# Banded attention inside an encoder layer: operands split once at projection, near maximum kept negated, far sums taken by a column of ones, far scores in alternating order

## The chip, the core and the metric

The kernel runs on one core of a Trainium2 chip. The core has five engines with instruction streams of their own: TensorE (PE; its weight loads are listed apart as PEld), VectorE (DVE), ScalarE (ACT), GpSimd (POOL) and SyncE (SP, which here only issues DMAs). Each engine takes its instructions in a fixed order. The order is made when the program is built: a scheduler takes the operations as the code emits them, with earlier ones preferred, and lays each on its engine where it expects the operands to be ready. Data lie in SBUF (128 partitions), in PSUM (where PE writes) and in DRAM.

The metric is the device time of one execution in microseconds. The kernel before takes 2369.29 us (median of three runs, 2369.18 to 2370.75).

## What is computed

The layer is a feed-forward block, a mixer and a second feed-forward block over 1024 tokens of width 1024. The mixer has eight attention heads of width 64 and an RWKV-7 group that shares the input projection. The attention is the part that the change touches:

```python
DILATED_PATTERNS = ((128, 1), (512, 4), (2048, 16))
...
    for window, dilation in DILATED_PATTERNS:
        o, l = _dilated_attention(q, k, v, window, dilation)   # o: softmax output, l: log of its denominator
...
    wts = jax.nn.softmax(jnp.stack(lses, axis=0), axis=0)
    o = jnp.sum(wts[..., None] * jnp.stack(outs, axis=0), axis=0)
    o = o * lax.rsqrt(jnp.mean(o * o, axis=-1, keepdims=True) + NORM_EPS)
```

In a pattern, query i sees the keys i + dilation*j with |j| up to window/(2*dilation). The mix of three softmaxes by their denominators equals one softmax over all keys of the three patterns, where a key that two patterns share counts twice.

## The kernel before

**Stages.** First feed-forward block; low-rank and value projections; projection and turning of queries and keys (`project_attention`); attention (`attention`); projection of the RWKV streams (`project_rwkv`); preparation and scan of the RWKV blocks; output projection; second feed-forward block. Attention and `project_rwkv` don't depend on each other, so the scheduler may lay the products of the second (tile `zr`, L510) between those of the first on PE. `project_rwkv` goes over eleven column blocks: the four key blocks, three of the four r blocks (the first was done in `project_attention`), and then, between preparations, the four value blocks. Each takes 48 products of 512 columns, 528 in all. Their weights come in pieces of 64 KB (`zraw`) on SP's queue.

**Two halves of a number.** A float32 operand is used as a high part (rounded to the fast format `F32R`) and a low part (the rest), made by a copy on ACT and a subtraction on DVE. The near scores are q times k from stacked halves: `sq` holds the high part of q in one half of the partitions and its low part in the other; `kh` holds the high part of k twice, `kl` its low part twice. One product of `sq` with `kh` and one with `kl` (L685, L686) then make the whole score. `stacked` (L654) builds the three for a head from the float32 q and k of its pair of heads, with three ACT copies (L660 to L662) and three DVE subtractions (L663 to L665) over 64 partitions by 1024.

**Turning (L472 to L489).** For each of eight token tiles of k and then of q: 24 products of 512 columns, a copy out of PSUM on ACT (L477), the rotation in three DVE operations (L480 to L482), four transposes on PE (L486), a DVE copy (L488) and a store to DRAM by POOL's queue (L489).

**Far keys (`far`, L619).** Dilation 16 splits tokens into 16 residues of 64. For each residue, PE multiplies 64 queries with 64 keys, read with a step of 16 elements (L626). The result of residue r goes to rows 0 to 63 of the PSUM tile for r below 8, and to rows 64 to 127 from 8 on. DVE takes the maximum and subtracts it, ACT takes the exponential, DVE sums (L632); PE transposes (L638); ACT copies; PE multiplies with the values (L644); output, maximum and sum go to DRAM as `n3` and come back by tokens as `far`.

**Near keys (`near`, L668).** Dilations 1 and 4 stay within 256 tokens. For each of eight query tiles, up to 640 keys: `scores` makes the products, and a DVE operation (L687) adds a table of logarithms of counts and takes the running maximum at once. DVE negates the maximum (L690), ACT takes exp(s - m) and sums (L691). `turn` transposes on PE (L700) and copies (L701, shared between ACT and DVE); `values` multiplies with the values (L707). The emission is staggered: scores of tile t, turn of t-1, values of t-2. At a head's end eleven small DVE and ACT operations (L720 to L730) merge the near and far softmax; a DVE product (L732) then empties the PSUM tile `po` that the next head's values need.

**Heads.** While head h runs, the code emits the three parts of `far(h + 1)` at tiles 1, 3 and 5, and `stack(h + 1)` at tile 4. Scores use two PSUM tiles (tag `s`, shared with the far work); `sq`, `kh` and `kl` have two buffers each, that is two heads.

Of the kernel before, what the change touches and what calls it, by code (L numbers as in the profile page):

```python
# [31 lines left out]
def _ap(src, off, pat):  # L32
    return bass.AP(tensor=src.tensor, offset=src.offset + off, ap=pat)
# [130 lines left out]
class _Kernel:  # L164
# [290 lines left out]
    def project_attention(self, p, psum, x, streams):  # L455
# [12 lines left out]
        for b in (1, 0):  # L468
            hl = self.columns(p, b * 512, 512, W[b], bufs=11)
            if b:  # L470
                self.load(rope.rearrange("p t a b c -> p t (a b c)"), self.io["k_rope"].rearrange("(t p) c -> p t c", p=128))
            for t in range(NT):  # L472
                ps = psum.tile([128, 512], F32, name="zq", tag="d", bufs=5)
                self.token_major(ps, x, t, hl)
                ts = slice(t * 128, t * 128 + 128)
                z = zz[t % 6]
                A.activation(z.rearrange("p a b c -> p (a b c)"), ps, AF.Copy, scale=HD ** -0.5 if b == 0 else 1.0)  # L477
                cs = rope[:, t]
                o, y = zo, zy
                V.tensor_tensor(o, z, cs[:, None, 0].to_broadcast([128, 8, 2, 32]), op=OP.mult)  # L480
# [138 lines left out]
    def far(self, psum, p, h, q, k, v3):  # L619
# [4 lines left out]
        ps = psum.tile([128, NT, 64], F32, name="s3", tag="s", bufs=2)  # L624
        for r in range(16):
            T.matmul(ps[row(r // 8), r % 8, :], q[hs, r::16], k[hs, r::16], start=True, stop=True)  # L626
        n3 = p.tile([128, NT, 66], F32, name="n3", tag="n3", bufs=1)
        s = p.tile([128, NT, 64], F32, name="sb3", tag="sb3", bufs=1)
        V.tensor_reduce(out=n3[:, :, 64], in_=ps, op=OP.max, axis=AX.X)
        V.tensor_tensor(s, ps, n3[:, :, 64:65].to_broadcast([128, NT, 64]), op=OP.subtract)  # L630
        A.activation(s, s, AF.Exp)
        V.tensor_reduce(out=n3[:, :, 65], in_=s, op=OP.add, axis=AX.X)  # L632
        yield
# [6 lines left out]
        yield  # L640
        po = [psum.tile([128, 4, 64], F32, name="po3" + tag, tag=tag, bufs=2) for tag in "st"]
        for r in range(16):
            c, g, j = r // 8, r % 8 // 2, r % 2
            T.matmul(po[j][row(c), g, :], e[row(j), g, row(c)], v3[row(j), c * 4 + g, hs], start=True, stop=True)  # L644
        for j in range(2):
            A.copy(n3[:, j::2, 0:64], po[j])
        for c in range(2):
# [5 lines left out]

    def stacked(self, p, h, q, k):  # L654

        V, A = self.nc.vector, self.nc.scalar
        hs, os = slice(h % 2 * 64, h % 2 * 64 + 64), slice(64 - h % 2 * 64, 128 - h % 2 * 64)
        sq, kh, kl = (p.tile([128, S], F32R, name=n, tag=n) for n in ("sq", "kh", "kl"))
        q, k = q[hs], k[hs]
# [3 lines left out]
        V.tensor_tensor(sq[os], q, sq[hs], op=OP.subtract)  # L663
        V.tensor_tensor(kl[hs], k, kh[hs], op=OP.subtract)
        V.tensor_tensor(kl[os], k, kh[hs], op=OP.subtract)  # L665
        return sq, kh, kl

    def near(self, psum, p, h, sq, kh, kl, v, far, between):  # L668

        nc, V, A, G, T = self.nc, self.nc.vector, self.nc.scalar, self.nc.gpsimd, self.nc.tensor  # L670
        hs = slice(h % 2 * 64, h % 2 * 64 + 64)
        m, nm, d, M, c12, c3 = (p.tile([128, NT], F32, name=n, tag=n) for n in ("m", "nm", "dn", "M", "c12", "c3"))
        po = psum.tile([128, NT, 64], F32, name="po", tag="o", bufs=1)
# [3 lines left out]
        def scores(t):  # L677
# [4 lines left out]
            for c in range(0, n, 512):  # L682
                e = min(n, c + 512)
                ps = psum.tile([128, 512], F32, name="s12", tag="s", bufs=2)
                T.matmul(ps[:, :e - c], sq[:, qs], kh[:, k0 * 128 + c:k0 * 128 + e], start=True, stop=False)  # L685
                T.matmul(ps[:, :e - c], sq[:, qs], kl[:, k0 * 128 + c:k0 * 128 + e], start=False, stop=True)  # L686
                V.tensor_tensor_reduce(out=s[:, c:e], in0=ps[:, :e - c], in1=bias[:, c:e], scale=1.0,  # L687
                                       scalar=m[:, t:t + 1] if c else -3e38, op0=OP.add, op1=OP.max,
                                       accum_out=m[:, t:t + 1])
            V.tensor_scalar(nm[:, t:t + 1], m[:, t:t + 1], -1.0, None, op0=OP.mult)  # L690
            A.activation(s[:, :n], s[:, :n], AF.Exp, bias=nm[:, t:t + 1], accum_out=d[:, t:t + 1])  # L691

# [25 lines left out]
        f = far  # L718
        fm, fd = f[:, :, 64], f[:, :, 65]
# [20 lines left out]
    def attention(self, psum, p):  # L740
        X, F, ST = {}, {}, {}

        def load(pr):
            v3 = p.tile([128, 8, 128], F32, name="v3", tag="v3", bufs=1)
            for j in range(2):
                self.load(v3[j * 64:j * 64 + 64],
                          _ap(self.v_att, j * 512 + pr * 128, [[16 * 512, 64], [2 * 512, 8], [1, 128]]))
            vn = p.tile([128, NT, 128], F32, name="vn", tag="vn")
# [12 lines left out]
        def stack(h):  # L761
            q, k, _, _ = X[h // 2]
            ST[h] = self.stacked(p, h, q, k)

# [334 lines left out]
    def constants(self):  # L1099
# [13 lines left out]
        self.ws_d = [self.dram(f"ws{j}", [4, NM, 128, 512]) for j in range(2)]  # L1113
        self.v_att, self.ya_d = self.dram("va", [S, 512]), self.dram("ya", [S, 512])
        self.n3_d = [self.dram(f"n3{j}", [S, 66]) for j in range(2)]
        self.lr_d = {nm: [self.dram(f"{nm}{d}", [4, 128, S]) for d in range(2)] for nm in "wa"}
# [319 lines left out]
```

## Time and profile before

| what | value |
|---|---|
| median of three runs | 2369.29 us |
| span of the profiled execution | 2367.7 us |
| mean granted clock of TensorE | 0.960 |
| products of the q and k projection | 801.5 to 902.9 us |
| first far scores | 918.4 us |
| first and last value product of the heads | 942.0 and 1163.5 us |
| products `zr` | 923.8 to 1261.0 us |
| first product of the RWKV preparation (L830) | 1208.2 us |

A row of a group gives the line in the code, the engine, the operation, the output and inputs by name, the shape, the count; then busy time in us and mean duration in ns; then the idle time of the engine before it and what ended that idle time. A row of the timeline begins with the start and the length in us. On PE a float32 product stands as two rows, so 16 far products are 32 rows; a run of rows is merged with its count.

### The profile page before, as it was taken

The page shows a single profiled execution, that of the slowest core. Times are in us where ns is not written, and L with a number is a line of the kernel's source. Part 1 is how long each engine was busy: PE and PEld are TensorE (multiplying, and loading weights), DVE is VectorE, ACT ScalarE, POOL GpSimd, SP SyncE. Part 2 cuts the span into 40 slices and gives each one's busy share as a digit, 9 for nine tenths or more (in the row PEclk, how much of TensorE's full clock was granted, in tenths as well). Part 3 has the DMA queues.
Part 4 walks back from the last instruction along what each step waited for, and adds up shares of the span by engine and source line. Part 5 has one row for each costly group of instructions (what it writes and reads, how often), then busy time and mean ns, then how long its engine had stood idle before and what let it go on. Part 6 is the DMA issues. An engine that isn't in the chain of part 4 may idle for free. (4 is left out here: it accounts for less than half of the span.)

```text
span 2367.7 us, 39507 instructions
## 1 busy us (share of the span) xinstructions
PE 2212.2 (93%) x14532; PEld 1784.9 (75%) x14532; DVE 1782.8 (75%) x2957; ACT 1034.4 (44%) x1958; POOL 608.7 (26%) x732
## 2 busy tenths in 40 slices
PE   6999999999999998999995889988799999999997
PEld 4788888878877676788774767765678888887886
DVE  8899999865676344667568767837889999987565
ACT  4322333354676413666545545445442333235453
POOL 6244443400000010111102242432334344441000
PEclk8999999999999998999996798989989999999999
DMA  5354445486652514322369676577534544447655
GB/s 156 107 174 151 170 146 170 167 266 193 220 185 98 193 42 134 91 81 71 94 161 223 165 183 176 151 208 256 178 95 168 174 167 154 169 153 265 195 188 181
DMA packets 359381, 386.04 MB, mean 163 GB/s; under 512 B 74258, under 2 KB 265618, under 8 KB 359188
## 3 DMA queue, kind: packets, MB, share of 16 engines
q1 hardware_dynamic: 308512, 276.43, 38.8%
q0 software_dynamic: 30320, 94.44, 11.3%
q10 hardware_dynamic: 20356, 12.66, 1.9%
q8 instruction: 114, 1.87, 0.3%
q14 instruction: 79, 0.65, 0.1%
HBM read 257.53 MB, written 125.89 MB: 162 GB/s over the span
## 5 line engine op out<-in xcount | busy, mean ns | idle before, releaser
L186 ACT ACTIVATE wh<-raw 128x512 fp32r<-128x512 f32 (+1 forms) x273 | 167.8, 626 | 264.1 <-DVE raw L62 95.0
L187 DVE TENSOR_TENSOR wl<-raw,wh 128x512 fp32r<-128x512 f32 (+1 forms) x273 | 277.6, 1020 | 3.1 <-ACT wh L186 2.0
L81 PE MATMUL gu<-xh,wh 128*128 128x512 f32 x704 | 277.9, 395 | 0.9 <-ACT xh L186 0.8
L81 PE MATMUL gu<-xl,wh 128*128 128x512 f32 x704 | 276.3, 393 | 0.0
L81 PE MATMUL gu<-xh,wl 128*128 128x512 f32 x704 | 276.2, 392 | 0.0
L415 PE MATMUL pd<-gl,gwh 128*128 128x512 f32 x616 | 240.4, 390 | 3.1 <-DVE gl L187 3.1
L415 PE MATMUL pd<-gh,gwh 128*128 128x512 f32 x616 | 239.6, 390 | 0.5 <-DVE row L86 0.5
L415 PE MATMUL pd<-gh,gwl 128*128 128x512 f32 x616 | 239.7, 389 | 0.0
L86 DVE TENSOR_TENSOR row<-gu,row 128x512 f32<-128x512 f32 x308 | 206.4, 682 | 23.2 <-PE gu L81 22.4
L187 DVE TENSOR_TENSOR gwl<-graw,gwh 128x512 fp32r<-128x512 f32 (+1 forms) x176 | 117.0, 667 | 129.7 <-ACT gwh L186 127.5
L116 POOL DMA_DIRECT2D d_hid<-row x154 | 84.7, 551 | 470.6 <-DVE row L114 444.2
L186 ACT ACTIVATE gwh<-graw 128x512 fp32r<-128x512 f32 (+1 forms) x176 | 101.4, 576 | 190.5 <-PE pd L415 162.2
L81 PEld LDWEIGHTS gu<-xh,wh 128*128 128x128 f32 x704 | 133.9, 190 | 29.5 <-ACT xh L186 2.0
L81 PEld LDWEIGHTS gu<-xl,wh 128*128 128x128 f32 x704 | 133.8, 190 | 27.9
L81 PEld LDWEIGHTS gu<-xh,wl 128*128 128x128 f32 x704 | 133.3, 189 | 27.5
L415 PEld LDWEIGHTS pd<-gl,gwh 128*128 128x128 f32 x616 | 115.6, 188 | 28.5 <-DVE gl L187 4.9
L415 PEld LDWEIGHTS pd<-gh,gwh 128*128 128x128 f32 x616 | 115.5, 188 | 25.6 <-DVE row L86 0.8
L415 PEld LDWEIGHTS pd<-gh,gwl 128*128 128x128 f32 x616 | 115.6, 188 | 23.8
L94 ACT ACTIVATE row<-row 128x512 f32<-128x512 f32 x44 | 27.9, 633 | 223.9 <-DVE row L86 216.4
L187 DVE TENSOR_TENSOR gl<-raw,gh 128x512 fp32r<-128x512 f32 x160 | 112.9, 717 | 15.7 <-ACT gh L186 15.4
L145 POOL TENSOR_TENSOR ws<-ws 128x512 f32<-128x512 f32 x88 | 114.4, 1300 | 1.2
L186 ACT ACTIVATE gh<-raw 128x512 fp32r<-128x512 f32 x160 | 98.0, 621 | 32.2 <-DMA raw<-in_ffn_w_down_dram 21.1
(356 smaller groups left out, 5353.4 us busy)
## 6 DMA issues: line engine op xcount, KB each, us to landing
d_hid<-row POOLq DMA_DIRECT2D x154, 256.0 KB, 2.5
graw<-d_hid SPq DMA_DIRECT2D x132, 256.0 KB, 3.0
raw<-in_ffn_w_gate_dram SPq DMA_DIRECT2D x88, 256.0 KB, 3.1
raw<-in_ffn_w_up_dram SPq DMA_DIRECT2D x88, 256.0 KB, 3.3
ws<-in_ffn_w_down_dram SPq DMA_DIRECT2D x88, 256.0 KB, 4.5
d_ws<-ws POOLq DMA_DIRECT2D x88, 256.0 KB, 2.3
raw<-d_ws SPq DMA_DIRECT2D x88, 256.0 KB, 2.7
raw<-in_ffn_w_down_dram SPq DMA_DIRECT2D x66, 256.0 KB, 3.3
```

The lines of the kernel that those rows point to most:

```text
L81: self.K.nc.tensor.matmul(ps, a[:, k, :], b[:, k, :], start=(k == 0 and i == 0), stop=(k == 3 and i == 2))
L86: add = lambda o, x: V.tensor_tensor(o, ps, x, op=OP.add)
L94: A.activation(y[:, 0], y[:, 0], AF.Silu)
L116: put = lambda n, y: G.dma_start(self.hid[n - 1, j // 2], y)
L145: G.tensor_tensor(o, a, b, op=OP.subtract)
L186: self.nc.scalar.activation(h, src, AF.Copy)
L187: (eng or self.nc.vector).tensor_tensor(l, src, h, op=OP.subtract)
L415: T.matmul(ps[x], a[:, ts], b, start=(m == 0 and k == 0), stop=(m == NM - 1 and k == 2))
```

## The change

- When q or k is turned, its high and low halves are made at once for all heads (one ACT copy and one DVE subtraction per token tile, from PSUM) and stored by SP to four new DRAM tensors. `stacked` becomes six loads of 256 KB per head on SP.
- The near maximum is kept as the negated minimum of the negated scores: L687 scales by -1 and takes the minimum; the negation L690 goes, and the exponential scales by -1. The merge is rewritten to fit, with the two factors in one tile.
- The far values get a 65th column of ones, so that the far product yields the sum; the DVE sum L632 goes. The value tile `v3` is loaded in four pieces of 64 columns instead of two of 128, and POOL sets the ones.
- The far scores go over the residues in the order 0, 8, 1, 9, and so on.

```diff
@@ project_attention
                 V.tensor_copy(y, q)
                 self.nc.gpsimd.dma_start((self.q_d, self.kt_d)[b][:, :, ts].rearrange("a p t -> p a t"), y)
+                hl = [p.tile([128, 4, 128], F32R, name="zs" + c, tag="zs" + c, bufs=2) for c in "hl"]
+                A.activation(hl[0], q, AF.Copy)
+                V.tensor_tensor(hl[1], q, hl[0], op=OP.subtract)
+                for c in range(2):
+                    self.load((self.qs_d, self.ks_d)[b][c][:, :, ts].rearrange("a p t -> p a t"), hl[c].bitcast(F32))
@@ far
-        for r in range(16):
+        for r in [c * 8 + g for g in range(8) for c in range(2)]:
             T.matmul(ps[row(r // 8), r % 8, :], q[hs, r::16], k[hs, r::16], start=True, stop=True)
...
-        V.tensor_reduce(out=n3[:, :, 64], in_=ps, op=OP.max, axis=AX.X)
-        V.tensor_tensor(s, ps, n3[:, :, 64:65].to_broadcast([128, NT, 64]), op=OP.subtract)
+        V.tensor_reduce(out=n3[:, :, 65], in_=ps, op=OP.max, axis=AX.X)
+        V.tensor_tensor(s, ps, n3[:, :, 65:66].to_broadcast([128, NT, 64]), op=OP.subtract)
         A.activation(s, s, AF.Exp)
-        V.tensor_reduce(out=n3[:, :, 65], in_=s, op=OP.add, axis=AX.X)
...
-            T.matmul(po[j][row(c), g, :], e[row(j), g, row(c)], v3[row(j), c * 4 + g, hs], start=True, stop=True)
+            T.matmul(po[j][row(c), g, :], e[row(j), g, row(c)], v3[row(j), c * 4 + g, h % 2, :], start=True, stop=True)
@@ stacked
-        A.activation(sq[hs], q, AF.Copy)
-        A.activation(kh[hs], k, AF.Copy)
-        A.activation(kh[os], k, AF.Copy)
-        V.tensor_tensor(sq[os], q, sq[hs], op=OP.subtract)
-        V.tensor_tensor(kl[hs], k, kh[hs], op=OP.subtract)
-        V.tensor_tensor(kl[os], k, kh[hs], op=OP.subtract)
+        pr, hs = h // 2, slice(h % 2 * 64, h % 2 * 64 + 64)
+        for half in range(2):
+            os = slice(half * 64, half * 64 + 64)
+            self.load(sq[os].bitcast(F32), self.qs_d[half][pr, hs])
+            self.load(kh[os].bitcast(F32), self.ks_d[0][pr, hs])
+            self.load(kl[os].bitcast(F32), self.ks_d[1][pr, hs])
@@ near
-                V.tensor_tensor_reduce(out=s[:, c:e], in0=ps[:, :e - c], in1=bias[:, c:e], scale=1.0,
-                                       scalar=m[:, t:t + 1] if c else -3e38, op0=OP.add, op1=OP.max,
-                                       accum_out=m[:, t:t + 1])
-            V.tensor_scalar(nm[:, t:t + 1], m[:, t:t + 1], -1.0, None, op0=OP.mult)
-            A.activation(s[:, :n], s[:, :n], AF.Exp, bias=nm[:, t:t + 1], accum_out=d[:, t:t + 1])
+                V.tensor_tensor_reduce(out=s[:, c:e], in0=ps[:, :e - c], in1=bias[:, c:e], scale=-1.0,
+                                       scalar=nm[:, t:t + 1] if c else 3e38, op0=OP.add, op1=OP.min,
+                                       accum_out=nm[:, t:t + 1])
+            A.activation(s[:, :n], s[:, :n], AF.Exp, bias=nm[:, t:t + 1], scale=-1.0, accum_out=d[:, t:t + 1])
...
-        V.tensor_tensor(M, m, fm, op=OP.max)
-        V.tensor_tensor(c12, m, M, op=OP.subtract)
-        V.tensor_tensor(c3, fm, M, op=OP.subtract)
-        A.activation(c12, c12, AF.Exp)
-        A.activation(c3, c3, AF.Exp)
+        V.scalar_tensor_tensor(M, fm, -1.0, nm, op0=OP.mult, op1=OP.min)
+        V.tensor_tensor(c12, M, nm, op=OP.subtract)
+        V.tensor_tensor(c3, fm, M, op=OP.add)
+        A.activation(cc, cc, AF.Exp)
...
-        V.tensor_tensor(c12, c12, d, op=OP.mult)
-        V.tensor_tensor(c3, c3, d, op=OP.mult)
+        V.tensor_tensor(cc, cc, d[:, None, :].to_broadcast([128, 2, NT]), op=OP.mult)
@@ attention, load
-            v3 = p.tile([128, 8, 128], F32, name="v3", tag="v3", bufs=1)
-            for j in range(2):
-                self.load(v3[j * 64:j * 64 + 64],
-                          _ap(self.v_att, j * 512 + pr * 128, [[16 * 512, 64], [2 * 512, 8], [1, 128]]))
+            v3 = p.tile([128, 8, 2, 65], F32, name="v3", tag="v3", bufs=1)
+            self.nc.gpsimd.memset(v3[:, :, :, 64:65], 1.0)
+            for c in range(2):
+                for j in range(2):
+                    self.load(v3[j * 64:j * 64 + 64, :, c, 0:64],
+                              _ap(self.v_att, j * 512 + pr * 128 + c * 64, [[16 * 512, 64], [2 * 512, 8], [1, 64]]))
```

More of the change, by code (lines that the diff above doesn't have):

```diff
@@ L468, in project_attention @@
         for b in (1, 0):
-            hl = self.columns(p, b * 512, 512, W[b], bufs=11)
+            w = self.columns(p, b * 512, 512, W[b], bufs=11)
             if b:
@@ L473, in project_attention @@
                 ps = psum.tile([128, 512], F32, name="zq", tag="d", bufs=5)
-                self.token_major(ps, x, t, hl)
+                self.token_major(ps, x, t, w)
                 ts = slice(t * 128, t * 128 + 128)
@@ L640, in far @@
         yield
-        po = [psum.tile([128, 4, 64], F32, name="po3" + tag, tag=tag, bufs=2) for tag in "st"]
+        po = [psum.tile([128, 4, 65], F32, name="po3" + tag, tag=tag, bufs=2) for tag in "st"]
         for r in range(16):
             c, g, j = r // 8, r % 8 // 2, r % 2
-            T.matmul(po[j][row(c), g, :], e[row(j), g, row(c)], v3[row(j), c * 4 + g, hs], start=True, stop=True)
+            T.matmul(po[j][row(c), g, :], e[row(j), g, row(c)], v3[row(j), c * 4 + g, h % 2, :], start=True, stop=True)
         for j in range(2):
-            A.copy(n3[:, j::2, 0:64], po[j])
+            A.copy(n3[:, j::2, 0:65], po[j])
         for c in range(2):
@@ L671, in near @@
         hs = slice(h % 2 * 64, h % 2 * 64 + 64)
-        m, nm, d, M, c12, c3 = (p.tile([128, NT], F32, name=n, tag=n) for n in ("m", "nm", "dn", "M", "c12", "c3"))
+        nm, d, M = (p.tile([128, NT], F32, name=n, tag=n) for n in ("nm", "dn", "M"))
+        cc = p.tile([128, 2, NT], F32, name="cc", tag="cc")
         po = psum.tile([128, NT, 64], F32, name="po", tag="o", bufs=1)
@@ L718, in near @@
         f = far
-        fm, fd = f[:, :, 64], f[:, :, 65]
-        V.tensor_tensor(M, m, fm, op=OP.max)
-        V.tensor_tensor(c12, m, M, op=OP.subtract)
-        V.tensor_tensor(c3, fm, M, op=OP.subtract)
-        A.activation(c12, c12, AF.Exp)
-        A.activation(c3, c3, AF.Exp)
+        fd, fm, c12, c3 = f[:, :, 64], f[:, :, 65], cc[:, 0], cc[:, 1]
+        V.scalar_tensor_tensor(M, fm, -1.0, nm, op0=OP.mult, op1=OP.min)
+        V.tensor_tensor(c12, M, nm, op=OP.subtract)
+        V.tensor_tensor(c3, fm, M, op=OP.add)
+        A.activation(cc, cc, AF.Exp)
         V.tensor_tensor(d, d, c12, op=OP.mult)
@@ L761, in stack @@
         def stack(h):
-            q, k, _, _ = X[h // 2]
-            ST[h] = self.stacked(p, h, q, k)
+            ST[h] = self.stacked(p, h)
         load(0)
@@ L1114, in constants @@
         self.v_att, self.ya_d = self.dram("va", [S, 512]), self.dram("ya", [S, 512])
+        for nm in "qk":
+            pool = self.pool(self.top, "d_s" + nm, space=DRAM)
+            setattr(self, nm + "s_d", [pool.tile([4, 128, S], F32, name=f"d_s{nm}{c}") for c in "hl"])
         self.n3_d = [self.dram(f"n3{j}", [S, 66]) for j in range(2)]
```

5 lines of the change are left out of this document (1 added, 4 removed).

## The prediction

> **What bounds the kernel now.** I read the page's header and busy shares first, then the chain of waits, then a table by stage, then the TensorE timeline inside the attention.
>
> ```profile
> span 2367.7 us, 39507 instructions
> PE 2212.2 (93%) x14532; PEld 1784.9 (75%) x14532; DVE 1782.8 (75%) x2957; ACT 1034.4 (44%) x1958; POOL 608.7 (26%) x732
> ...
> PE 26%; DVE 2%; issue 1%; DMA 1%; ACT 0%; POOL 0%; SPq 0%; DVEq 0%; POOLq 0%
> ```
>
> The profiled span is 2367.7 us against a median of 2369.29 for the runs: 1.6 us lie around it. The chain stops inside the second FFN (26% of the span on PE), so it doesn't reach the attention; stages must be read directly. The table holds the turn into attention, the eight heads, the projection after them, and the start of the scan preparation.
>
> ```profile
> 905.00:932.50 27.50, 17.92 (x117) 14.11 (x115) 14.32 (x18) 10.61 (x16) 1.30 (x2) 0.78 0.56 172
> 932.50:1163.70 231.20, 229.02 (x2361) 183.50 (x2359) 155.90 (x487) 146.99 (x345) 30.14 (x29) 0.99 0.30 82
> 1163.70:1203.00 39.30, 39.28 (x175) 32.20 (x172) 18.50 (x38) 16.19 (x43) 7.28 (x13) 1.00 0.43 133
> 1203.00:1262.00 59.00, 51.64 (x358) 41.03 (x358) 47.30 (x115) 32.21 (x67) 1.86 (x3) 0.97 0.81 204
> ```
>
> Columns are PE, weight loads, DVE, ACT, POOL, granted clock, DMA share, GB/s. In the eight heads PE is busy 229.0 of 231.2 us while DVE has 156 and ACT 147. So PE sets the pace there, and the DVE and ACT work that the change removes is covered. PE is full because the scheduler laid projection matmuls (tile zr) between those of the heads: 238 of their 528 stand before the last value product. These counts, here and below, are from the order of the built programs.
>
> **The change part by part.** *Turning.* Per token tile the projection gains one ACT copy, one DVE subtraction (16 each) and two stores on SP.
>
> ```profile
> L477 ACT ACTIVATE zz<-zq 128x512 f32<-128x512 f32 x16 | 9.6, 598 | 77.8 <-PE zq L440 77.8
> L480 DVE TENSOR_TENSOR zo<-zz,rope 128x512 f32<-128x512 f32 x16 | 11.1, 691 | 36.3 <-ACT zz L477 36.3
> d_q<-zts POOLq DMA_DIRECT2D x8, 256.0 KB, 2.5
> ```
>
> By these shapes that is 16 x 0.60 = 9.6 us of ACT and 16 x 0.69 = 11.1 us of DVE, under engines that idle 77.8 and 36.3 us there waiting for PE; without that cover it would be some 20 us. Only the last tile's 0.7 us and its stores (2.5 us to landing, by d_q) could show, and the next rows show the q load held by d_q anyway until 913.24.
>
> *Start of the heads.* Today ACT and DVE split two heads' q and k there, ahead of the first far softmax.
>
> ```profile
> 913.24 0.33 SPq L182 DMA_DIRECT2D qp<-d_q  x1
> ...
> 918.41 3.39 PE L626 MATMUL s<-kp,qp 64*64 64x64 f32 x32 [3.40 <-DMA kp<-d_kt]
> ...
> 919.73 2.47 DVE L663 TENSOR_TENSOR sq<-qp,sq 64x1024 fp32r<-64x1024 f32 x2
> ...
> 925.84 0.68 DVE L629 TENSOR_REDUCE n<-s 128x8 f32<-128x512 f32 x1
> ...
> 928.52 0.63 ACT L631 ACTIVATE sb<-sb 128x512 f32<-128x512 f32 x1 [4.76 <-DVE sb L630]
> ...
> 929.20 1.11 PE L638 MATMUL pt<-ident,sb 128*128 128x128 f32 x4 [3.75 <-ACT sb L631]
> ...
> 930.35 0.59 ACT L639 COPY e<-pt 128x512 f32<-128x512 f32 x1 [0.60 <-PE pt L638]
> ...
> 930.99 0.37 PE L644 MATMUL po3s<-v,e 64*64 64x64 f32 x1 [0.25 <-ACT e L639]
> ...
> 932.53 0.69 PE L685 MATMUL s<-kh,sq 128*128 128x384 f32 x1
> ```
>
> Without these splits the chain is far scores 918.4 to 920.4 (2.0, below), maximum and subtraction 0.68 each, exp 0.63, transposes 0.8 to their copy's start, copy 0.6, far values 1.54 (930.99 to 932.53), hand-offs 0.3: 925.6 instead of 932.5. In place of the splits stand loads of six 256 KB halves per head on SP. Behind them in SP's queue are zr's weight loads, so no zr matmul fills this start any more (five do today, 1.2 us). The loads must move 1.5 MB after q and k, while that stretch already runs at 356 to 393 GB/s:
>
> ```profile
> 913.41:916.83 3.42, 1.59 (x8) 0.98 (x6) 0.00 (x0) 2.02 (x4) 0.00 (x0) 1.00 0.74 236
> 916.83:920.24 3.41, 1.83 (x20) 1.86 (x21) 3.08 (x3) 3.34 (x5) 0.01 (x1) 1.00 1.07 356
> 920.24:923.66 3.42, 1.55 (x16) 1.36 (x13) 1.92 (x2) 3.35 (x4) 0.54 (x1) 0.50 1.05 393
> ...
> 930.48:933.90 3.42, 3.17 (x37) 2.25 (x36) 2.44 (x6) 1.11 (x3) 0.00 (x0) 0.50 0.10 24
> ```
>
> At 375 GB/s 1.5 MB take 4 us more, until 922 to 924: just in time. The half clock (0.50, four such windows) stays until PE fills a window, so part of the earlier work runs slow, some 1 us. I take 5 us saved; bounds 7 saved and 2 lost (loads at half that rate).
>
> *Far scores.* Sixteen 64x64 products per head, two rows each. All eight of one half of the output rows come first, then the other half.
>
> ```profile
> 1047.98 0.71 PE L700 MATMUL pt<-ident,sb 128*128 128x128 f32 x5
> 1048.62 0.80 PE L707 MATMUL po<-vn,e 128*64 128x64 f32 x20
> 1049.35 0.51 PE L510 MATMUL zr<-xh,zl 128*128 128x512 f32 x1
> 1049.69 0.60 PE L700 MATMUL pt<-ident,sb 128*128 128x128 f32 x4
> 1050.22 0.80 PE L707 MATMUL po<-vn,e 128*64 128x64 f32 x20
> 1050.95 1.56 PE L626 MATMUL s<-kp,qp 64*64 64x64 f32 x12
> 1052.45 0.68 PE L707 MATMUL po<-vn,e 128*64 128x64 f32 x14
> ...
> 1053.79 2.02 PE L626 MATMUL s<-kp,qp 64*64 64x64 f32 x20
> 1055.74 0.50 PE L685 MATMUL s<-kh,sq 128*128 128x512 f32 x1
> 1056.08 0.39 PE L686 MATMUL s<-kl,sq 128*128 128x512 f32 x1
> ```
>
> From start to next start, 12 rows of one half take 1.50 us (125 ns each) and the 20 that hold the change of halves 1.95 (98 ns). The value products L707, which alternate halves, take 0.73 for 20 (37 ns). At half clock L626 took 3.39 for 32, no longer than at full: it is not the array that is slow but the operands, read with a step of 16. At the change of halves the rows run in pairs:
>
> ```profile
> 1053.79:1054.31 0.52, 0.52 (x8) 0.52 (x9) 1.00 0.00 0
> ```
>
> Eight starts in 0.52 us, 65 ns each: two strided streams do overlap. Alternating throughout gives 32 x 0.06 + 0.1 = 2.0 us instead of 1.50 + 1.95 = 3.45. Saved 1.4 a head, 11 in all; bounds 0 (no overlap) and 8 x (3.45 - 32 x 0.037) = 18.
>
> The Trainium skill speaks against more: "SBUF — State Buffer", section "Door 1: The DMA port swizzle", puts SBUF in 16-byte lines and a penalty on each access that crosses to a new line, which a step of 64 bytes always does. The 125 ns agree. If that penalty held per partition, two streams over the same 64 partitions would share it and save nothing; the pairs at 65 ns speak against that.
>
> *Moved projection.* In the new order only 86 of the 528 zr matmuls stand before the last value product: 152 move behind the heads. Cost there and here:
>
> ```profile
> 1164.00:1202.50 38.50, 38.50 (x171) 31.86 (x170) 8.20 (x14) 1.00 0.44 135
> ```
>
> Dense they take 38.5/170 = 0.226 us; alone between other shapes 0.34 (1049.35 to 1049.69). Most stand in bursts today, so I take 0.04 saved each, 6 us; bounds 0 and 152 x 0.11 = 17. Three key blocks' norm chains (row squares, turns) move too. They wait on ACT and DVE, with zr queued behind them on PE; in the heads PE lost 2.2 us to all waits, so I add 1 us; bounds 0 and 6 (2 a chain).
>
> *Fewer fillers.* Head 0 gets no zr, head 1 eight, the later ones 9 to 17 each, where today it is 18 to 39 (8 in the last). What they covered may become idle. Per token tile PE does scores 0.57 (1055.74 to 1056.31) and a quarter of that for the last 128 keys, transposes 0.64, values 0.73. A tile's transposes come after the next tile's scores, so 0.71 + 0.64 + 0.73 + 0.71 = 2.8 us of PE work lie from its scores' start to them.
>
> ```profile
> L687 DVE CUSTOM_DVE_ANT_0 sb<-s,k_bias 128x512 f32<-128x512 f32 x48 | 33.0, 689 | 32.9 <-PE s L686 20.2 <-PE pt L700 8.4 <-ACT sb L691 1.5
> L691 ACT ACTIVATE sb<-sb,nm 128x640 f32<-128x640 f32 x32 | 26.5, 828 | 28.2 <-DVE nm L690 17.2 <-DVE zl L187 4.4 <-POOL ya L735 4.4
> L687 DVE CUSTOM_DVE_ANT_0 sb<-s,k_bias,m 128x128 f32<-128x128 f32 x32 | 11.1, 348 | 5.1 <-PE s L686 4.2
> L690 DVE TENSOR_SCALAR nm<-m 128x1 f32<-128x1 f32 x64 | 9.5, 149 | 1.1
> ```
>
> Against it stands the score pair 0.73, 0.69, 0.35, read-back 0.1, exp 0.83 and hand-offs 0.3: 3.0 without L690's 0.15. So 0.2 idle a tile, except in the three tiles per head that hold far work. Heads 0 and 1: 2 x 5 x 0.2 = 2; their ends, where the next values wait for the DVE product that frees their PSUM tile, 1 each; the second pair's q and k, now queued late on SP, 2; the six filled heads 0.5 each: 9 lost. Bounds 3 and 25 (0.3 on all 64 tiles and 0.8 at each end).
>
> *At nothing.* The negation L690 and the far sum (8 of a length like L629's) go, the eleven small operations of the merge become nine; all DVE and ACT under PE, save the 0.15 counted above. A minimum with scale -1 I price as the same row; a 65th column adds 1/64 to the far values, 0.1 us over all. The far value loads halve their runs: hidden, one head early.
>
> **Sum.** -5 - 11 - 6 + 1 + 9 = -12. After the heads the two orders agree almost wholly (zr ahead of the first preparation product: 414 and 416), so the end moves with them: 2367.7 - 12 + 1.6 = 2357 us.
>
> **The rivals.**
>
> *No overlap in the far scores*: the reading of the 64 shared partitions is the limit and the two halves take turns at it; -12 + 11 = -1, 2368 us. For it the identical reading rate at both clocks; against it the pairs. 0.12. (By the rule of "SBUF — State Buffer" of the Trainium skill this is the outcome.)
>
> *Late loads.* Slower than before. SP issues in order; the split halves of head h+1 wait for head h-1's buffers, and zr loads stand between that wait for rings which PE empties. If heads 2 to 7 each reach their first scores before the loads landed, PE stands still with all behind it. By kp's 4.8 us to landing each costs some 4:
>
> ```profile
> kp<-d_kt SPq DMA_DIRECT2D x4, 512.0 KB, 4.8
> ```
>
> 6 x 4 = 24, so -12 + 24 = +12, 2381 us. It decides once SP is held back over a head's length less issue and landing, 20 - 7 = 13 us; six loads of 256 KB at 82 GB/s of other traffic don't do that. 0.17.
>
> *Stalls hardly appear* and the pairs are closer: -5 - 15 - 8 + 4 = -24, 2345 us. That PE idles 2.2 us in 231 today says that the fill is ample. 0.10.
>
> **How the numbers follow.** The forecast has the remaining 0.61, with its own range 2348 to 2364. The range 2344 to 2374 leaves out most of the late loads and the tail of the best case. A measurement tells 0.2% (4.7 us) from no change: faster below 2364.6. Faster: 0.60 of the forecast, the 0.10 and nothing else, 0.70; same: 0.01 + 0.12 + 0.01 of the late loads, 0.14; slower: 0.16.
>
> **What would show it.** L626's successor 2.0 us a head when unbroken; first near scores near 926; last value product near 1100 to 1115; the first preparation product some 12 us ahead of today's 1208; PE idle in heads 0 and 1 with DVE and ACT as releasers. Idle before near scores released by DMA, or half-clock windows beyond the first head, would make the forecast wrong; so would far scores still at 100 ns.

## The result, and the profile after

The changed kernel takes 2392.39 us (median of four runs, 2389.83 to 2398.71) against 2370.02 us of the kernel before on the same chip: ratio 1.0103, interval 1.0085 to 1.0122. It is 22 us slower, where 12 us less were forecast. First the header of the page, then the table by stage (start of the heads, eight heads, what lies between them and the first preparation product).

```profile
span 2388.1 us, 39660 instructions
## 1 busy us (share of the span) xinstructions
PE 2209.9 (93%) x14532; PEld 1781.7 (75%) x14532; DVE 1758.7 (74%) x2869; ACT 1018.8 (43%) x1940; POOL 604.7 (25%) x736
```

```profile
905.00:930.90 25.90, 16.29 (x122) 13.11 (x120) 7.32 (x9) 4.65 (x8) 1.43 (x3) 0.79 0.90 249
930.90:1144.10 213.20, 188.42 (x2141) 148.56 (x2140) 109.18 (x351) 103.28 (x270) 25.46 (x27) 0.90 0.52 124
1144.10:1231.80 87.70, 85.08 (x412) 69.82 (x412) 43.53 (x91) 46.25 (x103) 9.17 (x19) 1.00 0.37 121
```

The engines have less to do, but PE is busy in only 188.4 of the heads' 213.2 us (229.0 of 231.2 before), at a mean clock of 0.90, with the DMA engines at 0.52 instead of 0.30. The first preparation product (L830) starts at 1231.8 us instead of 1208.2: the loss is all made by then. Behind the heads PE is full at full clock (85.1 of 87.7 us), but it has 330 zr products to do there instead of 176. This row of the same window gives 78.35/330 = 0.237 us each:

```profile
1144.10:1231.80 87.70, 78.35 (x330) 60.93 (x330) 15.73 (x27) 1.00 0.37 121
```

So the first question is what stops PE in the heads; what the moved products cost is counted further down. The view of waits from 915 to 1144 us (total, times, longest) says for PE, and for VectorE from 905 to 1165:

```profile
PE s L687 <- DVE sb L635: 12.9, 5, 3.2
PE s L631 <- DMA kp<-d_kt: 12.6, 2, 6.6
PE s L687 <- DVE nm L689: 4.1, 6, 1.0
```

```profile
DVE sb L635 <- DMA d_ya<-ya: 14.5, 5, 3.8
```

The first row is the key, and the fourth says what is behind it. L635 writes the far scores to `sb3`. The merged output `ya` of the head before has the same buffer (L730, tag `sb3`), and it isn't free until its store has landed in DRAM. One such place in order of time:

```profile
992.78 0.69 DVE L634 TENSOR_REDUCE n<-s 128x8 f32<-128x512 f32 x1 [0.80 <-PE s L631]
993.43 0.39 ACTq L737 DMA_DIRECT2D d_ya<-ya  x1
...
1001.49 0.69 DVE L635 TENSOR_TENSOR sb<-s,n 128x512 f32<-128x512 f32 x1 [3.84 <-DMA d_ya<-ya]
...
1002.32 0.45 PE L687 MATMUL s<-kh,sq 128*128 128x128 f32 x1 [3.20 <-DVE sb L635]
```

The store is issued at 993.43; at 1001.49, 8 us on, VectorE may go on. Until then no near maximum (L689) can pass, since VectorE works in order; both PSUM tiles of the scores stay full, and PE stands for 3.2 us. The issue-to-landing view (KB, median us; 905 to 1165 us) of the kernel before and then of the changed one:

```profile
kp<-d_kt SPq DMA_DIRECT2D x4, 512.0 KB, 4.8
d_ya<-ya ACTq DMA_DIRECT2D x7, 256.0 KB, 2.8
```

```profile
kp<-d_kt SPq DMA_DIRECT2D x4, 512.0 KB, 7.2
d_ya<-ya ACTq DMA_DIRECT2D x8, 256.0 KB, 6.3
```

The coupling by the buffer was there before and cost nothing: the store took 2.8 us. Now it takes 6.3 (both are medians of the five landings that each trace has). The single landings tell more. The stores issued at 959.95, 993.43 and 1020.59 us met at least five, two and three loads of halves in flight and took 10.1, 8.0 and 6.3 us; those at 1104.74 and 1146.15 us, near the end of the heads, met none and took 2.6 and 2.8 us. The store is issued by ACT's queue, the halves by SP's; yet it is slowed. (The Trainium skill, "DMA: Bandwidth & Descriptors", section "Rules for kernel authors", says that transfers of different issuing engines run on the same 16 engines and interleave; these rows agree.) The second wait is that for kp of the second pair of heads, from SP's and PE's timeline:

```profile
948.73 2.06 SPq L182 DMA_DIRECT2D v<-d_va  x3
...
953.26 0.36 SPq L182 DMA_DIRECT2D far<-d_n  x1
953.67 0.59 SPq L182 DMA_DIRECT2D v<-d_va  x1
954.31 0.62 SPq L182 DMA_DIRECT2D qp<-d_q  x1
...
954.97 0.43 SPq L182 DMA_DIRECT2D kp<-d_kt  x1
...
965.06 2.03 PE L631 MATMUL s<-kp,qp 64*64 64x64 f32 x32 [6.01 <-DMA kp<-d_kt]
```

v3 has one buffer, in use until the far values of head 1 at 948; q and k stand behind it on SP, and PE gets kp 10 us after its issue. Before, they had been issued at 914.57 us, ahead of any heads.

### The profile page after: what moved, and what is told of

It is laid out like the page before. It is cut to its first block, busy times and chain, and to the rows that moved or that the text cites. A ratio compares the mean times of both kernels' runs of the same rounds, so it can differ in the third digit from the quotient of the medians.

```text
span 2388.1 us, 39660 instructions
## 1 busy us (share of the span) xinstructions
PE 2209.9 (93%) x14532; PEld 1781.7 (75%) x14532; DVE 1758.7 (74%) x2869; ACT 1018.8 (43%) x1940; POOL 604.7 (25%) x736
```

## The experiments

Times are medians; ratios are to the kernel before on the same chip in the same session. There single runs of one kernel lie up to 26 us apart within one session (of before, 2358 to 2384 us), so ratios carry the verdicts, also between runs of different sessions, and traces, of one execution each, the places. 0.1% is 2.4 us. "Fill" is the count of zr products ahead of the last value product in the built order: 238 before, 86 in the changed kernel.

**e1: ya in its own buffer.**

```diff
-        y = p.tile([128, NT, 64], F32, name="ya", tag="sb3", bufs=1)
+        y = p.tile([128, NT, 64], F32, name="ya", tag="ya3", bufs=1)
```

> The changed kernel, in which the merged output ya gets a buffer of its own and no longer shares one with the far scores sb3. Theory A (traffic): the six loads of split halves per head slow the store of ya from 2.8 to 7.1 us, and VectorE stands in L635 for 12.9 us in five heads until that store has emptied the shared buffer; with its own buffer these waits go: 2374 to 2382 us, no L635 wait on the store. Theory B (fill): it's the missing projection products between the heads; the wait only moves to the next thing that is late: 2387 us or more.

Measured: 2373.57 us, ratio 1.0027 (1.0004 to 1.0050), fill 76. No L635 wait on the store is left, though it still takes 6.8 us. The windows of heads 2 and 3, changed kernel first, then e1:

```profile
991.30:1018.50 27.20, 24.00 (x278) 19.34 (x280) 13.29 (x44) 12.07 (x32) 3.57 (x5) 0.94 0.56 150
1018.50:1044.70 26.20, 23.74 (x276) 18.85 (x276) 13.37 (x44) 12.07 (x33) 3.18 (x4) 0.93 0.57 121
```

```profile
987.00:1008.50 21.50, 21.35 (x275) 17.51 (x277) 12.86 (x42) 11.66 (x30) 3.58 (x5) 1.00 0.74 188
1008.50:1029.80 21.30, 21.20 (x274) 17.09 (x274) 13.24 (x44) 12.17 (x33) 3.22 (x4) 1.00 0.68 143
```

With three and two zr products fewer a head lasts 5 to 6 us less, and the clock is whole. By the two ratios (1.0103 and 1.0027, intervals apart) one buffer of 2 KB per partition is worth 18 us: theory A, and more than PE's 12.9 us of wait alone, since the half clock that followed it goes too.

**e2 to e4: parts of the change alone.** e2 is the changed kernel with `stacked` as before and no halves stored; e3 is the kernel before with the split at the turning and the loads alone; e4 is the kernel before with

```diff
-        for r in range(16):
+        for r in [c * 8 + g for g in range(8) for c in range(2)]:
```

> The changed kernel with the split taken back: no halves stored at the turning, stacked() as before from qp and kp on ScalarE and VectorE; far order, negated maximum, column of ones stay. Built order: 218 of 528 zr products ahead of the last value product (86 in the changed kernel, 238 before). Theories A and B alike: the loss was all in the split, the far scores save 11 us: 2357 to 2363 us. Theory C (the other parts cost: four pieces of v3, minimum with scale -1, the merge): 2375 us or more.

> The kernel before with the split at the turning and the six loads per head alone. Theories A and B: the changed kernel's loss without the far scores' gain of some 11 us: 2398 to 2406 us. Theory C: 2368 to 2376 us. The order has 116 zr products ahead of the last value product.

> The kernel before with the far scores' order of residues alternated alone; 238 zr products stay ahead of the last value product. If the 1.4 us a head that the rows show stay in an interval where TensorE is full: 2357 to 2361 us. If the time is given back at the heads' ends or in later stages: 2366 us or more.

| run | us | ratio (interval) | first L830 product |
|---|---|---|---|
| e2, all but the split | 2354.75 | 0.9945 (0.9919 to 0.9970) | 1200.9 us |
| e3, split alone | 2389.90 | 1.0101 (1.0061 to 1.0141) | 1232.7 us |
| e4, far order alone | 2354.12 | 0.9952 (0.9932 to 0.9971) | 1203.3 us |

The far order alone gives 11 us (interval 7 to 16), and the eight heads of e4 last 220.7 instead of 231.0 us. The other small parts together (e2 against e4) are worth nothing that can be measured; theory C falls. The split alone costs 24 us, fewer than expected: gain and loss don't add. In e3 L635 waits 5.1 us in all for the store, in the changed kernel 14.5 us. The same bytes are loaded, but of the five stores of e3 whose landing is seen only two met halves in flight (10.1 and 3.7 us); the other three took 2.3 to 2.6 us. So what slows the store is not how many bytes a head loads, but whether it meets them. The far order makes no difference where the halves are loaded (1.0103 with it, 1.0101 without); that its saving went into the longer wait is likely, not shown, since e3 also has 116 zr products in the heads instead of 86. What makes up e3's 24 us was not taken apart.

**e5 and e9: the second pair's q and k.** Both are e1 with q and k ahead of v3 in `load`, e5 for all pairs, e9 for the later pairs only:

```diff
+            if pr:
+                self.load(q, self.q_d[pr])
+                self.load(k, self.kt_d[pr])
             v3 = p.tile([128, 8, 2, 65], F32, name="v3", tag="v3", bufs=1)
...
-            self.load(q, self.q_d[pr])
-            self.load(k, self.kt_d[pr])
+            if not pr:
+                self.load(q, self.q_d[pr])
+                self.load(k, self.kt_d[pr])
```

> Run e1 (ya in a buffer of its own, 2373.6 us) with one more edit: for each pair of heads q and k are loaded ahead of the values v3 instead of behind them. In e1 PE still waits 7.1 us for kp ahead of head 1's far scores, and the clock is at half for 10 us there. Theory A1: kp is late because SP issues it only after v3's loads, which wait until the far values have read the one buffer of v3: that wait and the half clock behind it go, 2361 to 2367 us. Rival A2: kp is late because the six loads of halves fill the DMA engines at that time: 2371 to 2376 us. Built order: only 43 zr products ahead of the last value product (76 in e1); if fill were what counts (theory B), it would be slower than e1.

> Run e1 (ya in a buffer of its own) with q and k loaded ahead of v3 for the later pairs of heads only; e5 had done it for the first pair too, whose values then stood ahead of head 0's halves (kh 10.4 us late). First near scores at 932 as in e1. Theory A1 (kp of the second pair is late because its load stands behind v3's on SP): the wait of 7.1 us ahead of head 1's far scores and the 10 us of half clock go, 2361 to 2368 us. Rival A2 (late by the traffic of the halves): 2371 to 2376 us. 42 zr products ahead of the last value product.

The 7.1 us that both expectations name are the first wait for kp in e1, at the start of the heads (924.36 us). The second pair's wait, the one meant, was 3.9 us (963.71 us), with 10 us of half clock around it.

e5: 2373.92 us, 1.0028 (1.0000 to 1.0057): a miss. For the first pair the values now stood ahead of head 0's halves, and PE waited 10.4 us for kh. e9 mends that: 2367.86 us, 1.0007 (0.9984 to 1.0030). The second pair's kp is issued at 938.37 instead of 955.73 us, its wait and the half clock behind it are gone, and head 1 lasts 21.4 instead of 28.6 us: A1, by the trace. In time it is 5 us by the ratios, whose intervals overlap. Two of its heads, the first without a zr product, the second with ten:

```profile
958.00:979.40 21.40, 19.39 (x264) 15.36 (x266) 12.63 (x41) 11.37 (x29) 3.31 (x4) 1.00 0.78 179
...
1022.40:1044.00 21.60, 21.46 (x274) 17.18 (x274) 13.55 (x45) 12.16 (x34) 3.38 (x5) 1.00 0.68 154
```

A head lasts 21.5 us either way: without fill PE idles 2.0 us of it. So here the price of a head without fill is 2 us, as the forecast had it; it is the store and the queue that it had missed. The row says something else too: ten products cost such a head nothing, for they fill its idle time. The last value product stands at 1105.6 us, inside the forecast's 1100 to 1115, but with 42 products ahead of it and not the forecast's 86.

**e6 and e11: fewer bytes.** kh and kl are loaded once a head; ScalarE copies them to the other 64 partitions. e6 is the changed kernel so, e11 is e1 so.

```diff
-            self.load(kh[os].bitcast(F32), self.ks_d[0][pr, hs])
-            self.load(kl[os].bitcast(F32), self.ks_d[1][pr, hs])
+            for kx, c in ((kh, 0), (kl, 1)):
+                if half:
+                    A.activation(kx[os], kx[0:64], AF.Copy)
+                else:
+                    self.load(kx[os].bitcast(F32), self.ks_d[c][pr, hs])
```

> The changed kernel (ya again in the shared buffer), with kh and kl loaded once per head and their second copies made by ScalarE from the first: four loads per head, 1.0 MB instead of 1.5. Theory A (traffic): the store of ya takes some 5 us instead of 7, the wait in L635 falls by half from 12.9 us to some 6: 2380 to 2387 us. Theory B (fill: 89 zr products ahead of the last value product, 86 in the changed kernel): 2389 to 2395 us.

> Run e1 with four loads per head instead of six (second copies of kh and kl by ScalarE, as in e6): 74 zr products ahead of the last value product. If the traffic costs more than the store of ya (kp late, the start of the heads): 2362 to 2369 us. If the store was all that the traffic delayed: 2371 to 2376 us, as e1 and as e6 (2372.3 us), in which the two edits were each alone.

e6: 2372.29 us, 1.0023 (0.9999 to 1.0048), 19 us below the changed kernel by the ratios and more than theory A had expected, with fill 89 as good as unchanged. The store's landing and VectorE's wait for it, in e6:

```profile
d_ya<-ya ACTq DMA_DIRECT2D x8, 256.0 KB, 3.7
```

```profile
DVE sb L635 <- DMA d_ya<-ya: 4.0, 4, 3.0
```

A third of the bytes taken away, and the store takes 3.7 us instead of 6.3, the wait 4.0 instead of 14.5. That it is the traffic of the halves that slows the store is shown by this run and by the single landings above. e11: 2364.69 us, 1.0001 (0.9975 to 1.0026): 6 us below e1 by the ratios, but their intervals overlap. That the traffic costs something beside the store is likely, not shown.

**e7, e10, e13, e14: the fill, by other queues.** In e7 (changed kernel) and e10 (e1) POOL issues the halves; in e13 (changed kernel) and e14 (e9) POOL issues the weights of zr.

```diff
-            self.load(sq[os].bitcast(F32), self.qs_d[half][pr, hs])
+            self.nc.gpsimd.dma_start(sq[os].bitcast(F32), self.qs_d[half][pr, hs])
```

```diff
-            self.load(raw, self.io["w_in"][0][k * 128:(k + 1) * 128, c0:c0 + n])
+            (queue or self.nc.sync).dma_start(raw, self.io["w_in"][0][k * 128:(k + 1) * 128, c0:c0 + n])
...
-            hl = self.columns(p, ATT + c0 * 128, n * 128)
+            hl = self.columns(p, ATT + c0 * 128, n * 128, queue=self.nc.gpsimd)
```

> The changed kernel with the six loads per head issued by POOL instead of SP: the same bytes, but the weights of zr no longer stand behind them, and the order has 169 zr products ahead of the last value product instead of 86. Theory B (fill): 2357 to 2366 us. Theory A (traffic): the same bytes slow the store of ya as before, the waits in L635 stay above 8 us in all: 2375 to 2390 us.

> Run e1 with the six loads per head on POOL's queue. As many zr products ahead of the last value product as in e1 (74, e1 76), but 12 of them in head 0 and 8 in head 1, where e1 has none. If what is left in e1 (some 18 us above run e2) is the first two heads without fill and at half clock: their lengths of 26.5 and 28.6 us fall to some 25 each with the fill in them, 2358 to 2366 us. If it lies elsewhere: 2370 to 2376 us.

> The changed kernel with one edit: the weights of the zr products are loaded by POOL's queue instead of SP's. Halves, shared buffer of ya and order of loads stay; 194 zr products stand ahead of the last value product (86 in the changed kernel). Theory B (the missing fill is the loss): 2355 to 2364 us. Theory A (the late store of ya stops VectorE and with it PE, whatever fill the order has): 2374 to 2386 us, with L635 waiting over 8 us in all for the store.

> Run e9 (ya in a buffer of its own, q and k of later pairs first; 2367.9 us) with the weights of zr on POOL's queue: 163 zr products ahead of the last value product (42 in e9). If the rest of the loss is fill, heads that take 21.5 us with 0 to 12 products now hold more of them at no cost: 2353 to 2361 us. If the loads of halves cost by themselves: 2365 to 2372 us.

e7: 2367.45 us, 1.0000 (0.9977 to 1.0023). It tells nothing apart: on POOL's queue the same bytes came at other times, the store took 3.8 us, L635 waited 3.4 us in all, and the fill was back too. e10: 2367.57 us, 1.0023 (0.9999 to 1.0047). Head 1 falls from 28.6 to 22.1 us, since kp of the second pair is no longer waited for, as in e9; but the first near scores start 3.1 us later (935.1 us), and head 0 takes 27.3 us with a wait of 5.3 us for kh. By the ratios e10 is as e1 (1.0023 and 1.0027), and the first preparation product comes at 1210.8 us, in e1 at 1211.6; the fill isn't told apart. e13: 2405.88 us, 1.0174 (1.0141 to 1.0208); e14: 2378.19 us, 1.0050 (1.0032 to 1.0068). Both are slower than either theory had it. One reason is in the start: the order now has zr ahead of the first far scores, and its weights come late (e13, ScalarE):

```profile
932.94 0.31 ACT L186 ACTIVATE zh<-zraw 128x128 fp32r<-128x128 f32 x1 [14.36 <-DMA zraw<-in_w_in_dram]
```

PE stands 16.8 us, and the first far scores start at 944.9 us instead of 923.3. By the first preparation product most of that is made good (1235.0 us against 1231.8 in the changed kernel, in e14 1210.2 against 1207.4 in e9); the rest of their loss lies later and stays open. What e13 does show: with fill 194, L635 still waits 16.7 us for the store, and PE 14.8 us behind it. Fill doesn't cover a wait of VectorE, because the scores behind it stand in PE's order too.

**e8: fewer products in the heads without any halves.** e2 with ya in its own buffer; the scheduler then puts 144 zr products into the heads instead of 218.

> Run e2 (split as before, 2354.8 us) with ya in a buffer of its own. With the split as before no load of halves stands in the store's way, it takes 2.9 us and no L635 wait shows: 2352 to 2357 us. If the shared buffer costs something even so (it ties the order of the heads' ends): 2345 to 2351 us. The order has 144 zr products ahead of the last value product (218 in e2); if fill counted, it would be slower, 2360 us or more.

Measured 2365.42 us, 0.9988 (0.9966 to 1.0010): 10 us more than e2 by the ratios, the outcome that the expectation gave to fill, and the first preparation product (L830 in the kernel before) at 1212.4 instead of 1200.9 us. The zr products between the last value product and that one, in e2 and in e8:

```profile
1153.20:1200.90 47.70, 44.92 (x196) 36.56 (x196) 9.04 (x16) 1.00 0.44 132
```

```profile
1133.00:1212.40 79.40, 66.82 (x272) 52.26 (x272) 13.17 (x23) 0.96 0.36 116
```

Taking 74 products out shortened the heads by 17.4 us (217.0 to 199.6 from the first near scores to the last value product) and made the stretch behind them 31.7 us longer, since two chains of key norms moved with them, PE waits there 6.6 us instead of 1.9, and zr takes 0.246 us each instead of 0.229. So a product is cheap in the heads and dear behind them. The same shows in what is left between e9 and e2 (15 us by the ratios). Here are the heads and the stretch behind them, of e2 and then of e9:

```profile
936.00:1153.00 217.00, 215.08 (x2340) 170.02 (x2338) 145.74 (x402) 144.24 (x330) 29.50 (x32) 1.00 0.30 83
1153.00:1200.90 47.90, 45.97 (x214) 37.52 (x209) 25.65 (x52) 23.08 (x59) 7.48 (x15) 1.00 0.43 131
```

```profile
930.50:1105.60 175.10, 165.89 (x2070) 130.50 (x2070) 103.94 (x337) 94.33 (x254) 24.14 (x25) 0.96 0.63 144
1105.60:1207.40 101.80, 98.73 (x488) 80.70 (x483) 50.53 (x104) 52.97 (x117) 10.46 (x22) 1.00 0.36 119
```

Over both stretches e9 takes 276.9 us and e2 264.9. PE works 264.6 us in e9 and 261.1 in e2, and it idles 12.3 us instead of 3.8. So of the 12 us, some 8.5 are idle time that the products no longer fill, and moving them saved PE no work. Against it stand 5.5 us that e9 starts earlier; the rest of the 15 us lies behind the first preparation product and was not followed.

**e16: the far order undone in e9.** Same diff as e4, backwards.

> Run e9 with the far scores in the order of before (all eight residues of one half first); the same 42 zr products. If a head there is bound by the chain of VectorE and ScalarE (21.5 us with 0 zr and with 12), the 1.4 us a head that the alternation saves on PE are worth nothing: 2366 to 2372 us. If PE's time counts as in e4: 2376 to 2382 us.

Measured 2374.57 us, 1.0051 (1.0027 to 1.0074), below the second range and above the first. By the ratios that is 10 us above e9, with intervals that just overlap; the first preparation product is 17 us later (1224.5 us). The last section shows where.

**e12 and e15: something faster than e2?** e12 is e2 with head 0 alone loaded as halves (only the first pair stored); e15 is e2 with zr's weights on POOL's queue, fill 278.

> Run e2 (split as before) but for head 0, whose halves come from DRAM: the halves of the first pair alone are stored at the turning (64 KB each per token tile) and loaded with six loads; heads 1 to 7 split on ScalarE and VectorE. The start of the heads is then that of the changed kernel (first near scores 931 to 932 instead of 936), without the loads that hold back the later heads. If those microseconds stay: 2348 to 2352 us. If the rest of the stage is bound by loads and fill anyway: 2354 to 2358 us, as e2.

> Run e2 (split as before) with the weights of zr on POOL's queue: 278 zr products ahead of the last value product (218 in e2). TensorE is full in e2's heads, so more fill only moves products: 2352 to 2358 us. If a product in the heads is cheaper than behind them, 60 more of them save some 3 to 6 us: 2347 to 2351 us.

e12: 2365.02 us, 0.9993 (0.9965 to 1.0021); its first near scores stand at 935.5, no earlier than e2's. e15: 2367.15 us, 1.0007 (0.9994 to 1.0021), with 9.4 us of PE waiting for weights at the start, though its first preparation product is only 1.5 us behind e2's (1202.4 us). Both are slower than either of their expectations, and why was not followed. Neither beats e2 and e4, which beat both kernels.

## Why the prediction was wrong

The sum's own terms put the first preparation product at 1208.2 - 12 = 1196.2 us. It came at 1231.8, 35.6 us later: the whole miss (2392.4 instead of 2357 us) is made by then, and it splits into three stretches.

| stretch | by the terms of the sum | measured | over |
|---|---|---|---|
| first near scores at | 932.5 - 5 = 927.5 us | 930.9 us | 3.4 |
| heads, to the last value product | 231.0 - 11 - 152 x 0.266 + 9 = 188.6 us | 212.9 us | 24.3 |
| behind them, to the preparation | 44.7 + 152 x 0.226 + 1 = 80.1 us | 88.0 us | 7.9 |

(0.266 is 0.226 and the 0.04 taken to be saved. By these terms the last value product would come at 1116 us, just outside the window that the prediction names.)

- *Start of the heads*, 5 us saved: 1.6 measured. The chain from far to near scores took 7.6 us, 7.2 in the forecast; but far scores began at 923.3 instead of 918.4.

```profile
909.94 0.36 SPq L182 DMA_DIRECT2D d_sqh<-zsh  x1
910.67 0.36 SPq L182 DMA_DIRECT2D d_sql<-zsl  x1
911.08 0.69 SPq L182 DMA_DIRECT2D k_bias<-in_k_bias_dram  x1
911.95 2.71 SPq L182 DMA_DIRECT2D v<-d_va  x4
...
916.09 0.38 SPq L182 DMA_DIRECT2D kp<-d_kt  x1
...
923.28 2.03 PE L631 MATMUL s<-kp,qp 64*64 64x64 f32 x32 [6.60 <-DMA kp<-d_kt]
```

  Half of the delay is SP's queue: kp was issued at 916.09 instead of 913.67 us, behind the last stores of halves and the pieces of v3, though d_q had landed at 912.2 us. The prediction put these stores at nothing. The other half is the landing, 7.2 us after issue instead of 4.7. The loads of halves were asked only whether they land in time, not what they do to the others.
- *Far scores*, 2.0 us a head: right. In the changed kernel 32 rows take 1.96 us:

```profile
931.50 2.03 PE L631 MATMUL s<-kp,qp 64*64 64x64 f32 x32
933.46 0.69 PE L688 MATMUL s<-kl,sq 128*128 128x384 f32 x1
```

  e4 has the 11 us in full. In the changed kernel they were not seen (e3 is as slow without them). The rival of no overlap is refuted. The row of 3.39 us that the prediction reads at half clock ran at full clock until 920.3 us; but the first 32 rows of e16, all at half clock and in the old order, took 3.40 us, so the reading holds. That the step of 16 is what makes a row slow was tested by no run.
- *Moved projection*, 6 saved and 1 lost: not so, the third stretch. For 154 more products (176 to 330) it grew by 43.3 us, where the terms had 35.4. The products took 37.9 us more (0.246 each, forecast 0.226). The norm chains of the three key blocks brought other PE work with them, 6.9 us instead of 1.5; the working had counted only their waits. And the 0.04 saved in the heads weren't there to be had: where PE idles, a product costs nothing (e9).
- *Fewer fillers*, 9 us lost: **the step that failed most**, the second stretch. The heads should have taken 189 us and took 213. The working priced the latencies between PE, VectorE and ScalarE, and these were right: 2 us a head without fill in e9, and e1's heads, with 76 products and no wait for the store, last 186.1 us where the same terms give 186. It priced no DMA but one, "the second pair's q and k, now queued late on SP, 2": 6.0 us of wait, and half clock behind it (5 us in time, e9, not clear of noise). And it named no store: the buffer that ya shares with the far scores, free 2.8 us after issue before and 6.3 now, cost 18 us (e1).
- *Late loads*, the rival at 2381 us and 0.17: nearest in size and in its signs, idle before near scores (12.9 us) and half clock beyond the first head (17 us from 961.2 us on, and three windows later). Its mechanism was not quite it. No wait of PE for the halves stands in the heads; they delayed what shares the DMA engines with them, and its deciding point (SP held back over a head's length) had nothing to do with that.
- *At nothing*: right for the small parts (e2 equals e4), not for the stores of halves.

Open stay what the split costs alone (e3), what happens behind the first preparation product in the runs with zr on POOL's queue, and whether e11's gain over e1 is real.

## What to carry to other kernels

A load that is "hidden" must be priced by what else moves at that time: list the transfers whose landing frees a buffer, stores too, with their slack, and ask what happens when each takes twice as long. Tiles of two stages that share one buffer tie a compute engine to a store; that is free only as long as the store is quick. Work that fills idle time costs nothing where it stands; moved to a stretch without idle time it costs its whole length. Where an engine is made faster, look for the wait that it runs into: there the gain goes.

## What the runs showed of the hardware

The clock. In windows of 3.41 us it goes to half not only behind an empty stretch. Two pairs of the changed kernel's windows:

```profile
1077.31:1080.72 3.41, 1.67 (x18) 1.39 (x19) 2.50 (x5) 0.63 (x1) 0.00 (x0) 1.00 0.14 41
1080.72:1084.13 3.41, 3.41 (x17) 2.23 (x15) 2.38 (x5) 2.03 (x4) 0.59 (x1) 0.50 0.00 0
```

```profile
1227.50:1230.91 3.41, 1.64 (x10) 1.38 (x10) 3.41 (x8) 3.33 (x8) 0.53 (x1) 1.00 0.06 19
1230.91:1234.33 3.42, 3.31 (x36) 2.78 (x36) 2.53 (x6) 2.11 (x6) 0.00 (x0) 1.00 0.94 282
```

Behind 1.67 us of PE in the heads the clock was at half for a window (0.50); behind 1.64 us, six dense zr products and four transposes, it was not. So a wait of 2 us can cost more than itself, and the busy time alone doesn't say when. (The Trainium skill, "TensorE: Matmul & The Clock Gate", section "Part 1: The HAM clock gate (the "warmup" mystery)", names an idle window as the condition; the first pair was half busy.)

More surprising is e16. Its windows show PE busy without a gap, and yet half clock follows:

```profile
984.33:987.74 3.41, 3.41 (x42) 3.14 (x40) 0.95 (x3) 0.00 (x0) 2.73 (x3) 0.99 1.05 227
987.74:991.16 3.42, 3.20 (x9) 1.81 (x9) 2.66 (x6) 1.08 (x3) 0.53 (x1) 0.50 1.01 261
```

```profile
985.03 2.74 PE L631 MATMUL s<-kp,qp 64*64 64x64 f32 x26
```

That window held 2.7 us of far scores in the old order, 64x64 products at 105 ns a row with operands read in steps of 16. In e9, with the rows in pairs, the clock stays whole in the same heads. Head 1 lasts 24.2 us in e16 and 21.4 in e9, 2.8 us more, where the rows alone give 1.4; the half clock is the likely cause of the rest. The old order isn't needed for it. In e12 a window that PE fills, with sixteen products of two columns in 1.92 us and no far scores, is followed by half clock too:

```profile
1144.90:1148.31 3.41, 3.41 (x33) 2.81 (x31) 1.17 (x6) 1.59 (x6) 0.00 (x1) 1.00 0.39 159
1148.31:1151.72 3.41, 3.41 (x40) 2.79 (x40) 1.25 (x6) 2.17 (x4) 0.06 (x1) 0.50 0.00 0
```

```profile
1145.10 1.92 PE L592 MATMUL kn<-k_ones,ksq 128*128 128x2 f32 x16
```

These windows fit a clock that follows what the array computes and not how long it is occupied. That is a reading of the traces; no kernel made for it tested it.
